# Hybrid mLSTM and differential attention block: q and k of four attention heads as seven block products each, rotated in the pairs' stage and kept in DRAM

## The chip, the cores and the metric

One core of a Trainium2 chip (trn2) runs the whole block. The metric is the time of one execution on the device, in microseconds (us); lower is better. The engines are TensorE (PE), VectorE (DVE), ScalarE (ACT), GpSimd (POOL) and SyncE (SP), which issues nearly all transfers. Each engine takes its instructions in order and waits for the others by semaphores.

## What is computed

One layer for a sequence of 1024 rows of width 1024, in float32. After a root-mean-square norm, one wide projection gives twelve segments. Five of them (a_q, a_k, a_v, a_o, a_z) and the gates a_g feed an mLSTM with 4 heads in two directions; b_q, b_k, b_v and b_z feed a differential attention with 8 heads; g_a and g_b gate the two branches. What the change touches is the attention's q and k:

```
dq = apply_rope(b_q.reshape(B, S, 8, 2, 64), positions)   # rotation of the halves (t1, t2) of 64:
dk = apply_rope(b_k.reshape(B, S, 8, 2, 64), positions)   # t1 cos - t2 sin, t2 cos + t1 sin
p = softmax(dq dk^T * 64 ** -0.5)          # for each head two maps j = 0, 1
out = (p[0] - lam * p[1]) @ da_v           # then a norm and a gate with b_z
```

## The kernel before

Every large product is made of float32r matmuls in three terms: each operand is split into a high part H and a low part L, and HH, HL and LH are added in PSUM. A projection of 128 columns by 512 rows of the sequence takes 8 slices of the depth times 3 terms, 24 matmuls with 512 columns.

*Stages.* First the norm, the transposed input (`hH`, `hL`, one tile for each half of the sequence) and four early z projections. Then the **pairs' stage**: two projections of 128 columns and both halves of the sequence and of the depth are a 2 x 2 by 2 x 2 block product, for which `pair_units` takes seven products instead of eight, of 4 x 3 = 12 matmuls each, in Winograd's form, from sums of blocks of the input (`TH`, `TL`) and of the weights. `load_form` makes the weight forms: a sum or difference on POOL, a cast to H on ACT (L354), and L by a subtraction on POOL or DVE (L358). The form of a pair's product f waits in one of six buffers until a product before is done. Products 0, 1, 2 and 6 of a pair add up in one PSUM bank, so product 6 waits until ACT has copied the sum after product 2 away (`u3`, L392). Product 6 and product 5 of a pair are issued among the next pair's. When two or three products have come together, a **sink** finishes a block (i, j): i is the one of the two projections, j the half of the sequence. Before, there are 2 wide pairs for v of the mLSTM, 16 pairs that alternate between the convolution's sink (four POOL instructions each, L560) and the o and z sink (none on POOL), and 3 gate pairs.

*The attention stage.* The plain projections of q and k of one head are `da_proj`: kA is the weight of the first halves (t1) of q and k side by side, kB that of the second (t2), each for both halves of the sequence, 96 matmuls in all (L607). `first` multiplies kA's result by cos and sin (DVE, L1045 and L1046), `second` does kB's (L1056 and L1057); POOL adds and splits (L1058 to L1062, six instructions) and SP copies the parts into `kst` and `qq` (L1067), eight copies of two instructions' worth of rows for each half.

A head then has 8 steps t. In each, `scores` makes 12 matmuls S (L1126; two of them run at once on halves of the array), DVE takes two maxima (L1129), ACT two exponentials (L1131), which free the two PSUM tiles of S, and DVE the difference e (L1137). `transposes` makes 8 transposes T of the e of the step before, ACT and DVE split them (pH L1150, pL L1151), and every second step `pv` multiplies two steps by v (L1162, 24 matmuls). There is one set of PSUM tiles for S and two banks for T, PV and the small products.

*What sets the order.* PE's order is fixed by the program (`Weaver`). It gives every unit a cost, and names after which it may come, with a delay (`LAG`): S of a head comes 14 us after the head's projection, T 6.8 us after its S. `weave` merges the head's own units with a list of other work: q and k of the next head, v of the next two heads (`da_v`, after the last PV of the head before), z of the heads that aren't early. The other engines' and SP's order is made by a scheduler from this program.

Of the kernel before, what the change touches and what calls it, by code (L numbers as in the profile page):

```python
# [38 lines left out]
Z_EARLY = (0, 1, 3, 5)  # L39
MM = 0.214  # L40
# [88 lines left out]
class Block:  # L129
# [126 lines left out]
    def pair_raws(self, p):  # L256
        if p >= len(self.pairs) or p in self.praws:
            return
        self.praws[p] = raws = []
        if self.pairs[p][0] == "v":  # L260
            pool = self.wpool if p % 2 == 0 else self.s0
            for b in range(2):
                t = pool.tile([128, 8, 128], F32, name="raw", tag="raw", **({} if p % 2 == 0 else dict(bufs=2)))
                raws.append({0: wide(t)})
                self.load_piece(p, b, 0)
            for b in (1, 0):
                self.praws[p][b][1] = self.kit[(0, 4)[p % 2] + 1 - b].rearrange("p (k e) -> p k e", e=256)
                self.load_piece(p, b, 1)
            return
        for seg, i in self.pairs[p]:  # L270
# [50 lines left out]
    def load_form(self, key):  # L321
# [5 lines left out]
        r1, r2 = self.praws[p]  # L327
# [4 lines left out]
        lo, hi = slice(0, 4), slice(4, 8)  # L332
        tmp = lambda n: self.s0.tile([128, 4, 128], F32, name=n, tag=n, bufs=1)
        sub = lambda out, x, y: g.tensor_tensor(out=out, in0=x, in1=y, op=ALU.subtract)
        if f == 0:
            src = r1[:, lo]
        elif f == 1:
            self.s2f = src = tmp("s2f")
            sub(src, self.s1f, r1[:, lo])
        elif f == 2:  # L340
            src = self.s13[:, hi]
            sub(src, r1[:, lo], r2[:, lo])
        elif f == 3:
            self.s13 = self.s0.tile([128, 8, 128], F32, name="s13", tag="s13", bufs=1)
            self.s1f = src = self.s13[:, lo]
            g.tensor_tensor(out=src, in0=r2[:, lo], in1=r2[:, hi], op=ALU.add)
        elif f == 4:
            src = r1[:, hi]
        elif f == 5:
            src = self.s2f  # L350
            sub(src, r1[:, hi], src)
        else:
            src = r2[:, hi]
        cast = a.copy(H, src)  # L354
# [3 lines left out]
        (self.v if f in (0, 4, 6) else g).tensor_tensor(out=Lo, in0=src, in1=H.bitcast(F32), op=ALU.subtract)  # L358
# [148 lines left out]
    def gate_sink(self, i0):  # L507

        def sink(i, j, ps, rest):
# [7 lines left out]
            self.q.dma_start(out=self.tg["gb"][i0 + i][:, j * 512:(j + 1) * 512], in_=th)  # L517
        return sink
# [516 lines left out]
    def da_proj(self, h, st):  # L1035
# [73 lines left out]
    def da_parts(self, h, st):  # L1109
# [79 lines left out]
        def scale(half):  # L1189
# [10 lines left out]
            S=lambda t: Unit(6 * MM, lambda: scores(t), tag="S", hold=LAG["Sh"], name=("S", h, t), after=((("qk", h), LAG["qk"]),)),  # L1200
# [480 lines left out]
    def build(self):  # L1681
# [21 lines left out]
        with pool(name="const", bufs=1) as self.const, \  # L1703
# [20 lines left out]
            self.vd = {x: [[self.dram.tile([128, 512], F32, name=f"av{x}{n}_{c}") for c in range(NC)] for n in range(NH_A)] for x in "HL"}  # L1724
            self.zd = {h: self.dram.tile([128, S], F32, name=f"zd{h}") for h in Z_EARLY}
# [4 lines left out]
            for n in range(NH_A):  # L1730
                for i, seg in enumerate(("ak", "aq")):
# [3 lines left out]
                    sinks.append(self.oz_sink(2 * n + i))  # L1735
            for n in range(0, 6, 2):
# [181 lines left out]
```

## Time and profile before

| | |
|---|---|
| median of 3 runs (lowest to highest) | 1648.4 us (1648.01 to 1649.74) |
| the profiled execution | 1648.9 us |
| its span, first to last instruction | 1647.1 us |
| mean granted clock of PE | 0.999 |
| DVE, ACT, POOL: share of the span | 63%, 48%, 41% |
| moved by DMA | 208.15 MB, mean 126 GB/s |

The profile is of one execution. A row of the timeline has the start in the span, the length, engine, line, operation, what it writes and reads, and in brackets how long the engine stood before it and what ended that. A row of a group has the busy time, the mean length of one in ns, and the idle time before. Matmuls are pipelined: one is longer than the distance to the next. The stages, by the profile: the pairs' stage until about 530 us, attention from there to about 1160, then the mLSTM and the output.

### The profile page before, as it was taken

What the parts mean: (1) busy time and instruction counts of PE and PEld (TensorE: products, weight loads), DVE (VectorE), ACT (ScalarE), POOL (GpSimd) and SP (SyncE); (2) the same over time, 40 slices, a digit from 0 to 9 for tenths busy, and PEclk for the clock granted to TensorE, in tenths of its full rate; (3) what the DMA queues carried; (4) which work ended last, traced back from release to release, by engine and by line L of the source; (5) the groups of instructions that cost most, each with busy time, mean ns of one, the idle gap of its engine ahead of it and who ended that gap; (6) DMA issues with size and microseconds to landing.
All of it is one profiled execution on the core that took longest, in us unless ns stands there. A gap on an engine that the chain in (4) does not pass through costs nothing.

```text
span 1647.1 us, 25481 instructions
## 1 busy us (share of the span) xinstructions
PE 1616.7 (98%) x9299; PEld 1364.3 (83%) x9299; DVE 1045.8 (63%) x1866; ACT 787.8 (48%) x1602; POOL 674.1 (41%) x725
## 2 busy tenths in 40 slices
PE   7999999999999999999999999999999999999998
PEld 6899778878888988987888888888898888888887
DVE  5734787786771377677767776764167867456633
ACT  6433545555553254455445444554357666442221
POOL 3744676666774446243515344322322322222000
PEclk9999999999999999999999999999999999999999
DMA  5433444343443323222222131311697863466522
GB/s 186 151 127 131 119 135 148 115 141 116 146 129 109 103 54 89 65 64 78 54 72 63 46 77 39 91 52 52 200 307 260 270 190 130 145 227 216 179 101 78
DMA packets 193167, 208.15 MB, mean 126 GB/s; under 512 B 12313, under 2 KB 143730, under 8 KB 193042
## 3 DMA queue, kind: packets, MB, share of 16 engines
q1 hardware_dynamic: 189826, 200.75, 39.5%
q10 hardware_dynamic: 3216, 5.78, 0.9%
q8 instruction: 73, 1.20, 0.3%
q14 instruction: 52, 0.43, 0.1%
HBM read 128.79 MB, written 60.92 MB: 115 GB/s over the span
## 4 chain that ended last, share of the span: by engine, by line
PE 66%; DVE 4%; ACT 2%; DMA 2%; POOL 1%; issue 1%; SPq 0%; POOLq 0%; DVEq 0%; ACTq 0%
PE pj L607 27%; PE T L385 9%; PE T L1162 6%; PE S L1126 5%; PE pj L1631 5%; PE T L159 5%; PE pj L629 5%; PE T L155 2%; PE I L155 1%; PE SS L155 1%; PE PO L155 1%; DMA raw<-in_w_in_dram 1%; DMA ya<-gA 0%; DVE e L1137 0%; DVE hL L1517 0%
## 5 line engine op out<-in xcount | busy, mean ns | idle before, releaser
L607 PE MATMUL pj<-hH,wH 128*128 128x512 f32 x672 | 274.4, 408 | 0.1
L607 PE MATMUL pj<-hH,wL 128*128 128x512 f32 x672 | 263.8, 393 | 0.8 <-POOL wL L244 0.8
L607 PE MATMUL pj<-hL,wH 128*128 128x512 f32 x672 | 263.0, 391 | 0.6 <-DVE hL L763 0.6
L1129 DVE TENSOR_REDUCE nm<-S 128x1 f32<-128x1024 f32 x128 | 150.7, 1219 | 108.7 <-PE S L1126 108.7
L607 PEld LDWEIGHTS pj<-hH,wL 128*128 128x128 f32 x672 | 126.1, 188 | 29.4 <-POOL wL L244 2.1
L1131 ACT ACTIVATE e<-S,nm 128x1024 f32<-128x1024 f32 x128 | 142.7, 1130 | 7.0 <-DVE nm L1129 7.0
L607 PEld LDWEIGHTS pj<-hL,wH 128*128 128x128 f32 x672 | 126.7, 189 | 21.7 <-DVE hL L763 1.5
L607 PEld LDWEIGHTS pj<-hH,wH 128*128 128x128 f32 x672 | 126.6, 188 | 20.2 <-ACT hH L762 0.5
L1150 ACT CAST pH<-T 128x512 fp32r<-128x512 f32 x128 | 68.8, 588 | 147.4 <-PE T L159 147.4
L246 POOL TENSOR_TENSOR wL<-raw,wH 128x1024 fp32r<-128x1024 f32 x27 | 66.6, 2466 | 121.2 <-ACT wH L238 121.2
L1126 PE MATMUL S<-kst,qq 64*128 64x512 f32 x768 | 106.2, 408 | 0.0
L385 PE MATMUL T<-TH,wL 128*128 128x512 f32 x304 | 101.2, 394 | 2.4 <-ACT u L392 2.3
L385 PE MATMUL T<-TH,wH 128*128 128x512 f32 x304 | 101.0, 392 | 0.1
L1137 DVE SCALAR_TENSOR_TENSOR e<-e,r,e 128x1024 f32<-128x1024 f32 x64 | 93.5, 1461 | 1.8
L1126 PEld LDWEIGHTS S<-kst,qq 64*128 64x128 f32 x768 | 67.3, 184 | 29.2 <-issue 9.4
L551 DVE SCALAR_TENSOR_TENSOR pj<-cin,cols,pj 128x512 f32<-128x512 f32 x128 | 87.1, 745 | 0.0
L1151 DVE TENSOR_TENSOR pL<-T,pH 128x512 fp32r<-128x512 f32 x128 | 82.0, 680 | 6.1 <-ACT pH L1150 6.1
L224 POOL TENSOR_TENSOR wL<-raw,wH 128x512 fp32r<-128x512 f32 x32 | 47.0, 1485 | 79.8 <-ACT wH L223 79.8
L607 PE MATMUL pj<-sl_yb,wH 128*128 128x512 f32 x256 | 78.9, 389 | 0.0
L385 PE MATMUL T<-hH,wH 128*128 128x512 f32 x232 | 76.5, 391 | 0.2 <-DVE cin L532 0.2
L1333 POOL TENSOR_SCALAR_AFFINE_SELECT W<-gb 128x128 f32<-128x128 f32 (+1 forms) x64 | 26.3, 414 | 122.9 <-DVE W L1383 87.0
L385 PE MATMUL T<-hH,wL 128*128 128x512 f32 x224 | 74.5, 392 | 0.7 <-DVE oz L491 0.7
(405 smaller groups left out, 4449.4 us busy)
## 6 DMA issues: line engine op xcount, KB each, us to landing
raw<-in_w_in_dram SPq DMA_DIRECT2D x84, 512.0 KB, 4.0
kst<-hl SPq DMA_DIRECT2D x64, 128.0 KB, 2.4
qq<-hl SPq DMA_DIRECT2D x64, 128.0 KB, 2.4
x<-in_x_dram SPq DMA_DIRECT2D x8, 512.0 KB, 5.7
avH<-tz SPq DMA_DIRECT2D x16, 256.0 KB, 2.0
cak<-y SPq DMA_DIRECT2D x16, 256.0 KB, 2.7
cakH<-cin SPq DMA_DIRECT2D x16, 256.0 KB, 4.8
cakL<-tz SPq DMA_DIRECT2D x16, 256.0 KB, 4.6
```

What stands on the lines that cost most here:

```text
L155: self.t.matmul(out, lhsT=l, rhs=r, start=(i == 0), stop=(i == n - 1))
L159: self.t.transpose(out, in_, self.ident[0:k, 0:k])
L385: self.t.matmul(ps, lhsT=l[:, k, :], rhs=r[:, k, :], start=(first and k == 0 and m == 0), stop=(k == 3 and m == 2), skip_group_check=not f ...
L551: v.scalar_tensor_tensor(out=acc, in0=raw[:, o + x:o + x + 512], scalar=w(x), in1=acc, op0=ALU.mult, op1=ALU.add)
L607: self.t.matmul(ps, lhsT=l[:, k, :], rhs=r, start=(n == 0), stop=(n == 23))
L629: self.t.matmul(ps[:, i, :], lhsT=l, rhs=r[:, k, :], start=(kh == 0 and k == 0 and m == 0), stop=(kh == 1 and k == 3 and m == 2))
L1126: self.t.matmul(ps[:, o], lhsT=qq[r, x, c], rhs=k[r, y, o], start=(m == 0), stop=(m == 2))
L1129: v.tensor_reduce(out=nm, in_=ps, axis=AX.X, op=ALU.max, negate=True)
L1131: a.activation(out=e, in_=ps, func=AF.Exp, bias=nm[:, 0:1], accum_out=Z[:, j, t:t + 1])
L1137: v.scalar_tensor_tensor(out=e0, in0=e, scalar=r[:, 0:1], in1=e0, op0=ALU.mult, op1=ALU.add)
L1162: self.t.matmul(ps[:, 0:256], lhsT=l[:, k, :], rhs=r[:, i, :], start=(k == 0 and m == 0), stop=(k == 7 and m == 2))
L1631: self.t.matmul(ps, lhsT=x[:, s], rhs=y[:, c], start=(k == 0 and m == 0), stop=(k == 7 and m == 2))
```

## The change

For heads 0, 2, 4 and 6 the plain projections kA and kB in the attention stage are gone. In their place each has a pair `("rope", h)` in the pairs' stage, after the 16 mLSTM pairs and before the gate pairs. The two projections of the pair are kA and kB; its weights are loaded in two pieces by halves of the depth, with q's and k's 128 columns side by side, and the forms read them in groups of 32 columns. The new `rope_sink` adds the parts, multiplies by cos and sin (DVE), adds (POOL), casts (ACT) and subtracts (DVE), and SP writes H and L to a tensor `rd` in DRAM. In the attention stage `load_qk` loads `kst` and `qq` of such a head from `rd`, k and the first half of q at the start of the head before, the second half of q after its step 3. S of these heads then comes at least 5 us after the second load by the planner, instead of 14 after a projection. The other heads are as before.

```
+R_EARLY = (0, 2, 4, 6)
...
+        if self.pairs[p][0] == "rope":
+            vw = lambda x: x.rearrange("p k (g i) -> p k g i", i=32)
+            part = lambda b, kh: wide(self.praws[p][kh]).rearrange("p k (g t i) -> p k g t i", t=2, i=32)[:, :, :, b, :]
...
+    def rope_sink(self, h):
+        v, a, p, box = self.v, self.a, self.p, {}
+        def sink(i, j, ps, rest):
+            c = slice(j * 512, (j + 1) * 512)
+            if rest is not None:
+                to = self.psA.tile([128, 512], F32, name="pj", tag="pj", bufs=2) if i == j == 1 else ps
+                v.tensor_tensor(out=to, in0=ps, in1=rest, op=ALU.add)
+                ps = to
+            t = box[i, j] = self.big("rot")[:, 0:S]
+            v.tensor_tensor(out=t[:, 0:512], in0=ps, in1=(self.sinT if i else self.cosT)[:, c], op=ALU.mult)
+            v.tensor_tensor(out=t[:, 512:S], in0=ps, in1=(self.cosT if i else self.sinT)[:, c], op=ALU.mult)
+            if (1 - i, j) not in box:
+                return
+            x, H = box[0, j], box[1, j]
+            p.tensor_tensor(out=x[:, 0:512], in0=x[:, 0:512], in1=H[:, 0:512], op=ALU.subtract)
+            p.tensor_tensor(out=x[:, 512:S], in0=H[:, 512:S], in1=x[:, 512:S], op=ALU.add)
+            a.copy(H.bitcast(F32R), x)
+            v.tensor_tensor(out=x.bitcast(F32R), in0=x, in1=H, op=ALU.subtract)
+            for n, y in enumerate((H, x)):
+                self.q.dma_start(out=self.rd[h][:, :, n, c], in_=y.rearrange("p (x s) -> p x s", x=2))
+        return sink
...
+        def load_qk(half):
+            if half == 0:
+                st["k"] = w1.tile([128, 2, S], F32R, name="kst", tag="kst", bufs=2)
+            st["q", half] = w1.tile([128, 2, 512], F32R, name="qq", tag="qq", bufs=3)
+            for x in range(2):
+                for j in range(2):
+                    r, g = 64 * j + 32 * x, 32 * j
+                    if half == 0:
+                        q.dma_start(out=fb(st["k"][r:r + 32]), in_=self.rd[h][64 + g:96 + g, x])
+                    q.dma_start(out=fb(st["q", half][r:r + 32]), in_=self.rd[h][g:g + 32, x, :, half * 512:half * 512 + 512])
...
         qk = []
-        for half in range(2):
+        if h in R_EARLY:
+            qk = [Unit(0.0, lambda: load_qk(0)), Unit(0.0, lambda: load_qk(1), name=("qk", h), after=((("S", h - 1, 3), 1.0),), lane=1)]
+        for half in range(0 if h in R_EARLY else 2):
             qk += self.proj(kA, half, lambda ps, half=half: first(half, ps))
...
-            S=lambda t: Unit(..., name=("S", h, t), after=((("qk", h), LAG["qk"]),)),
+            S=lambda t: Unit(..., name=("S", h, t), after=((("qk", h), 5.0 if h in R_EARLY else LAG["qk"]),)),
...
+            for h in R_EARLY:
+                self.pairs.append(("rope", h))
+                sinks.append(self.rope_sink(h))
```

The order that comes of it, at three places. PE, between the last S of head 0 and the first of head 1 (`S<-kst,qq`; `ident,e` are transposes T, `pj<-hH,wH` a projection, `T<-pH,vH` PV, `ident,att` the small transposes). Before, the end of it:

```order
L607 MATMUL pj<-hH_195,wH 128x512
L607 MATMUL pj<-hL_196,wH 128x512
L607 MATMUL pj<-hH_195,wL 128x512
L1126 MATMUL S<-kst,qq 128x512 x12
L159 MATMUL T<-ident,e_5919 128x128 x8
L607 MATMUL pj<-hH_195,wH 128x512
```

In the change, all of it and what follows:

```order
L1179 MATMUL S<-kst,qq 128x512 x12
L160 MATMUL T<-ident,e_6290 128x128 x8
L647 MATMUL pj<-hH_201,wH 128x512
L647 MATMUL pj<-hL_202,wH 128x512
L647 MATMUL pj<-hH_201,wL 128x512
L160 MATMUL T<-ident,att 128x128 x2
L1179 MATMUL S<-kst,qq 128x512 x12
L160 MATMUL T<-ident,e_6368 128x128 x8
L1215 MATMUL T<-pH,vH 128x256
L1215 MATMUL T<-pL,vH 128x256
L1215 MATMUL T<-pH,vL 128x256
```

Before, 42 projection matmuls stand between the two S and 12 more between T and PV; in the change three, the last of head 1's projection, and none.

POOL, in the pairs' stage (`s`, `s2f`: sums for weight forms; `wH<-s`, `wL<-s2f`: their low parts; `y<-y,cin` a convolution's sink, `rot<-rot` the rope sink). Before, one pair's turn:

```order
L346 TENSOR_TENSOR s_4415<-raw 128x512
L334 TENSOR_TENSOR s_4415<-raw 128x512
L358 TENSOR_TENSOR wH<-s_4415,wH 128x512
L560 TENSOR_TENSOR y<-y,cin 128x512 x2
L358 TENSOR_TENSOR wL<-s2f,wL 128x512
L334 TENSOR_TENSOR s2f<-s_4415,raw 128x512
L358 TENSOR_TENSOR wH<-s2f,wH 128x512
L334 TENSOR_TENSOR s2f<-raw,s2f 128x512
L560 TENSOR_TENSOR y<-y,cin 128x512
```

In the change, a rope pair's turn:

```order
L351 TENSOR_TENSOR s_5048<-raw 128x512 x2
L552 TENSOR_TENSOR rot<-rot 128x512
L553 TENSOR_TENSOR rot<-rot 128x512
L374 TENSOR_TENSOR wH<-s_5048,wH 128x512
L552 TENSOR_TENSOR rot<-rot 128x512
L553 TENSOR_TENSOR rot<-rot 128x512
L374 TENSOR_TENSOR wL<-s2f,wL 128x512
L351 TENSOR_TENSOR s2f<-s_5048,raw 128x512
L374 TENSOR_TENSOR wH<-s2f,wH 128x512
```

Four sink instructions stand in one turn in both, in the change two ahead of the first low part and two behind it, and so in four turns running.

SP, around the copies of head 1's second half (`kst<-hl`, `qq<-hl`), in the change (before, `kst<-hl` and `qq<-hl` stand there alone, behind a weight load):

```order
L202 DMA raw<-in_w_in_dram 128x8x128
L1124 DMA kst<-rd_167 32x2048 x3
L1107 DMA kst<-hl 32x2x512 x2
L1107 DMA qq<-hl 32x2x512 x2
L1107 DMA kst<-hl 32x2x512 x2
L1107 DMA qq<-hl 32x2x512 x2
L1125 DMA qq<-rd_167 32x2x512 x3
```

Three loads of head 2's k, into the buffer that head 0's k leaves, stand ahead of them.

More of the change, by code (lines that the diff above doesn't have):

```diff
@@ L269, in pair_raws @@
             return
+        if self.pairs[p][0] == "rope":
+            pool = self.wpool if p % 2 == 0 else self.s0
+            for kh in range(2):
+                t = pool.tile([128, 8, 128], F32, name="raw", tag="raw", **({} if p % 2 == 0 else dict(bufs=2)))
+                for i, seg in enumerate(("bq", "bk")):
+                    o = OFF[seg] + 128 * self.pairs[p][1]
+                    src = self.A["w_in"][0][512 * kh:512 * kh + 512, o:o + 128]
+                    self.q.dma_start(out=wide(t)[:, :, 128 * i:128 * i + 128], in_=src.rearrange("(k p) e -> p k e", p=128))
+                raws.append(t)
+            return
         for seg, i in self.pairs[p]:
@@ L326, in load_form @@
             self.pair_raws(1)
-        r1, r2 = self.praws[p]
+        if self.pairs[p][0] == "rope":
+            vw = lambda x: x.rearrange("p k (g i) -> p k g i", i=32)
+            part = lambda b, kh: wide(self.praws[p][kh]).rearrange("p k (g t i) -> p k g t i", t=2, i=32)[:, :, :, b, :]
+        else:
+            vw = lambda x: x
+            part = lambda b, kh: self.praws[p][b][:, 4 * kh:4 * kh + 4]
         tag = "wH" if self.forms % 2 == 0 else "wL"
@@ L331, in load_form, with sub @@
         H, Lo = t[:, 0:4], t[:, 4:8]
-        lo, hi = slice(0, 4), slice(4, 8)
         tmp = lambda n: self.s0.tile([128, 4, 128], F32, name=n, tag=n, bufs=1)
-        sub = lambda out, x, y: g.tensor_tensor(out=out, in0=x, in1=y, op=ALU.subtract)
+        def sub(out, x, y, op=ALU.subtract):
+            g.tensor_tensor(out=vw(out), in0=x, in1=y, op=op)
+            return vw(out)
         if f == 0:
-            src = r1[:, lo]
+            src = part(0, 0)
         elif f == 1:
-            self.s2f = src = tmp("s2f")
-            sub(src, self.s1f, r1[:, lo])
+            self.s2f = tmp("s2f")
+            src = sub(self.s2f, vw(self.s1f), part(0, 0))
         elif f == 2:
-            src = self.s13[:, hi]
-            sub(src, r1[:, lo], r2[:, lo])
+            src = sub(self.s13[:, 4:8], part(0, 0), part(1, 0))
         elif f == 3:
             self.s13 = self.s0.tile([128, 8, 128], F32, name="s13", tag="s13", bufs=1)
-            self.s1f = src = self.s13[:, lo]
-            g.tensor_tensor(out=src, in0=r2[:, lo], in1=r2[:, hi], op=ALU.add)
+            self.s1f = self.s13[:, 0:4]
+            src = sub(self.s1f, part(1, 0), part(1, 1), ALU.add)
         elif f == 4:
-            src = r1[:, hi]
+            src = part(0, 1)
         elif f == 5:
-            src = self.s2f
-            sub(src, r1[:, hi], src)
-        else:
-            src = r2[:, hi]
-        cast = a.copy(H, src)
+            src = sub(self.s2f, part(0, 1), vw(self.s2f))
+        else:
+            src = part(1, 1)
+        cast = a.copy(vw(H), src)
         if f in (1, 5):
             self.behind(self.pins.get("u"), cast)
-        (self.v if f in (0, 4, 6) else g).tensor_tensor(out=Lo, in0=src, in1=H.bitcast(F32), op=ALU.subtract)
+        (self.v if f in (0, 4, 6) else g).tensor_tensor(out=vw(Lo), in0=src, in1=vw(H.bitcast(F32)), op=ALU.subtract)
         self.wt[key] = (H, Lo)
@@ L517, in sink @@
             self.q.dma_start(out=self.tg["gb"][i0 + i][:, j * 512:(j + 1) * 512], in_=th)
+        return sink
[11 more added lines that the diff above has]
+            if (1 - i, j) not in box:
+                return
+            x, H = box[0, j], box[1, j]
[5 more added lines that the diff above has]
+                self.q.dma_start(out=self.rd[h][:, :, n, c], in_=y.rearrange("p (x s) -> p x s", x=2))
         return sink
@@ L1199, in da_parts @@
         return dict(
-            S=lambda t: Unit(6 * MM, lambda: scores(t), tag="S", hold=LAG["Sh"], name=("S", h, t), after=((("qk", h), LAG["qk"]),)),
+            S=lambda t: Unit(6 * MM, lambda: scores(t), tag="S", hold=LAG["Sh"], name=("S", h, t), after=((("qk", h), 5.0 if h in R_EARLY else LAG["qk"]),)),
             T=lambda t, g: Unit(4 * TP, lambda: transposes(t, g), tag="T", hold=LAG["Th"], name=("T", h, t, g),
@@ L1724, in build @@
             self.vd = {x: [[self.dram.tile([128, 512], F32, name=f"av{x}{n}_{c}") for c in range(NC)] for n in range(NH_A)] for x in "HL"}
+            self.rd = {h: self.dram.tile([128, 2, 2, S], F32, name=f"rd{h}") for h in R_EARLY}
             self.zd = {h: self.dram.tile([128, S], F32, name=f"zd{h}") for h in Z_EARLY}
```

## The prediction

> **What bounds the kernel now.** I read the page first, then the chain of work, then the timeline around two heads of the attention stage, then the groups of instructions of the pairs' stage.
>
> ```profile
> PE 1616.7 (98%) x9299; PEld 1364.3 (83%) x9299; DVE 1045.8 (63%) x1866; ACT 787.8 (48%) x1602; POOL 674.1 (41%) x725
> 461.48 62.63 PE T L385 x276
> 530.50 21.76 PE pj L607 x96
> 552.26 15.83 PE pj L629 x132
> ```
>
> TensorE (PE) is the bound: busy in 98% of the span, no other engine above 63%. The two pieces of the chain give the price of a matmul of 512 columns. 276 of the pairs' stage took 62.63 us and 96 of a projection 21.76 us, so 0.227 us each (the 408 ns in the page's groups is one matmul's length in a pipeline, not its pace). The 96 are head 0's whole q and k projection; the third piece is v, 0.12 us for each matmul of 256.
>
> So two things can change the time: how many matmuls there are, and whether PE still always has one whose operands are there. The attention stage shows how it has that now.
>
> ```profile
> 636.20:708.40 72.20, 71.55 (x530) 63.04 (x529) 51.53 (x72) 37.22 (x82) 28.07 (x29) 1.00 0.20 53
> 776.90:855.10 78.20, 78.20 (x560) 68.28 (x559) 53.27 (x75) 37.27 (x82) 29.15 (x30) 1.00 0.21 55
> ```
>
> These are the stretches from the first score product of heads 1 and 3 to that of the next head (PE, weight loads, VectorE (DVE), ScalarE (ACT), GpSimd (POOL), granted clock, DMA). PE is full, DVE is busy for 52 to 53 us. One step t of a head is a chain through three engines:
>
> ```profile
> 787.13 1.66 PE L1126 MATMUL S<-kst,qq 64*128 64x512 f32 x12
> 788.72 1.09 PE L159 MATMUL T<-ident,e 128*128 128x128 f32 x8
> 788.83 2.36 DVE L1129 TENSOR_REDUCE nm<-S 128x1 f32<-128x1024 f32 x2 [3.57 <-PE S L1126]
> 791.48 1.13 ACT L1131 ACTIVATE e<-S,nm 128x1024 f32<-128x1024 f32 x1
> 791.10 1.28 DVE L1151 TENSOR_TENSOR pL<-T,pH 128x512 fp32r<-128x512 f32 x2
> 793.23 1.28 DVE L1137 SCALAR_TENSOR_TENSOR e<-e,r,e 128x1024 f32<-128x1024 f32 x1
> ```
>
> With the score product S at 0: PE is free for the transposes T of the step before at 1.6; they take 1.09 with the tail of the last one, so the next matmul can start at about 2.5. The second exponential ends at 5.5, and only then are S's banks free for the next S. The weights e of this step are ready at 7.4. The low parts pL of the transposed ones are written at 4.0 to 5.3, since DVE does the two maxima first, so the product PV can't begin before about 4.6. Between 2.5 and 4.6 to 5.5 PE needs other work: the projections of the next head and v.
>
> **The change part by part.** *Matmuls.* Four heads lose 96 each and four pairs gain 7 x 12 = 84 each: 48 fewer, 48 x 0.227 = **-10.9 us**. The work also moves: 4 x 84 x 0.227 = 76.3 us come to the pairs' stage, 21.8 go from the front of the attention stage, and 3 x 21.8 = 65 from the heads before 2, 4 and 6, where they were PE's other work. The rotation's products on DVE and POOL move with them.
>
> *Head 0 to head 1.* Head 1 is not among the four, so its projection still runs beside head 0. Now nothing follows it: the planner used to put 42 matmuls of head 2's projection (9.5 us) between it and head 1's first S, and those are gone, while v for heads 2 and 3 must wait for head 0's last PV. What that S waits for is here:
>
> ```profile
> 620.39 0.39 PE L607 MATMUL pj<-hH,wL 128*128 128x512 f32 x1
> 623.77 1.66 PE L1126 MATMUL S<-kst,qq 64*128 64x512 f32 x12
> 632.89 1.23 SPq L1067 DMA_DIRECT2D kst<-hl  x2
> 636.17 1.65 PE L1126 MATMUL S<-kst,qq 64*128 64x512 f32 x12
> kst<-hl SPq DMA_DIRECT2D x64, 128.0 KB, 2.4
> 600.60 1.29 POOL L1058 TENSOR_TENSOR m<-m,hl 128x512 f32<-128x512 f32 x1 [14.34 <-DVE hl L1056]
> 605.70 1.29 POOL L1062 TENSOR_TENSOR hl<-m,hl 128x512 fp32r<-128x512 f32 x1
> 607.71 1.23 SPq L1067 DMA_DIRECT2D kst<-hl  x2
> ```
>
> Head 1's last projection matmul ends at 620.8; the last k copies are issued at 632.9 to 634.1, and the second, issued at 633.5, lands 2.4 later at 635.9 at the latest (an estimate from the median). S comes at 636.17, so this delay of some 15 us was covered, barely. In the change the last three projection matmuls stand behind S(7) and T, and end at 1.6 + 0.9 + 0.7 = 3.2, plus 0.4 of pipeline; behind them PE has two short transposes and then head 1's S, at 3.5. DVE does maxima and pL until 5.3 and then the first product with sin, 5.9. POOL's six instructions took 6.4 us in the undisturbed half at 600.60; one low part of a rope weight now stands among them, 1.4. That is 13.7. From POOL's end to the last landing are 0.7 of issue wait, 0.6 between the two issues and 2.4: 17.4. PE waits 17.4 - 3.5, about **+14 us**. From below 11, if the weight's low part and DVE's order cost nothing; from above 17, since SP now stands with three loads of head 2's k, which wait for head 0's last S, ahead of these copies.
>
> *The heads 1, 3, 5.* Their only other work is now v, 192 matmuls, which may begin after the last PV of the head before. In step 0, and again in step 6 when v is used up, the order is S, T, PV with nothing between: PE stands from 2.5 to 4.7, 2.2 us. In step 6 DVE also has two parts of v and a gate product of the step before ahead of the maxima, about 0.6 more. That is 2.2 + 2.8 = 5.0 per head, **+15 us** for three. Below: 9, if DVE is ahead; above: 20, with 0.7 more at the ends of heads 2 and 4 and a late e.
>
> *The rope pairs.* Four pairs follow one another whose sinks put four instructions on POOL (L1058's kind). Of the pairs before, only every second did.
>
> ```profile
> L346 POOL TENSOR_TENSOR s<-raw 128x512 f32<-128x512 f32 x19 | 28.2, 1483 | 1.4
> L358 POOL TENSOR_TENSOR wH<-s2f,wH 128x512 fp32r<-128x512 f32 x20 | 26.0, 1299 | 32.4 <-ACT wH L354 32.4
> L354 ACT CAST wH<-raw 128x512 fp32r<-128x512 f32 x28 | 17.4, 620 | 6.4 <-PE pj L879 3.3 <-PE T L435 2.2 <-PE T L385 0.9
> L238 ACT CAST wH<-raw 128x1024 fp32r<-128x1024 f32 x41 | 43.1, 1052 | 43.7 <-PE pj L607 26.7 <-DMA raw<-in_w_in_dram 9.1 <-issue 6.5
> L1045 DVE TENSOR_TENSOR m<-pj,cosT 128x512 f32<-128x512 f32 x16 | 11.0, 690 | 14.2 <-PE pj L607 11.8 <-POOL hl L1062 2.4
> L358 DVE TENSOR_TENSOR wL<-raw,wL 128x512 fp32r<-128x512 f32 x29 | 31.0, 1073 | 4.5 <-ACT wL L354 4.5
> ```
>
> POOL's own time per pair is 8 weight-form instructions of 1.35 and 4 of 1.3, 16.0 of the pair's 84 x 0.227 = 19.1. But in its order it also waits: after the first two rotations for ACT's copy of 1024 and two casts (1.05 + 2 x 0.62 = 2.3), then for DVE's subtraction, a low part, a sum and a product beyond that (about 1.4), after the next two for ACT's copy and a cast (1.7), and once more for a cast (0.7). 16.0 + 6.1 = 22.1 is 3 us more than PE needs, and ACT's copy u of the third product, which PE's seventh waits for, stands behind. Three of four pairs would each lose 3: 9. If casts and sinks slip past one another as in the conv pairs, nothing. The order of the change shows them in a row, so I take **+7.5**, from 0 to 14 (a subtraction of 1024 at twice 1.07 instead of 0.69 adds 1.5 per pair).
>
> *PE's pace after a long wait.* The trace of before has no gap of over 3 us once PE runs, but its beginning shows slow matmuls:
>
> ```profile
> 0.00:15.00 15.00, 6.48 (x30) 5.08 (x30) 5.77 (x23) 7.61 (x11) 7.51 (x19) 1.00 0.87 315
> 8.24 1.54 PE L159 MATMUL T<-ident,x 128*128 128x128 f32 x6 [2.33 <-DVE rsv L693]
> 13.81 0.88 PE L159 MATMUL T<-ident,x 128*128 128x128 f32 x6 [0.19 <-DVE x L705]
> ```
>
> The same six transposes take 1.54 us after PE stood for 8 us with little work, and 0.88 five microseconds later, while the granted clock of these 15 us (the last column but two) is 1.00: it doesn't show this. S and T after the 14 us wait (2.5 us) would take 2.5 x 1.54 / 0.88 = 4.3: **+1.8 us**, between 0 and 4. The Trainium skill's page "TensorE: Matmul & The Clock Gate" (Part 1: The HAM clock gate) says that the array falls to half its clock after one idle window of about 3.4 us and needs as long a stretch of work to come back; by that rule the wait costs up to half of 3.4, 1.7 us (an estimate from the page's figure), more than its length, a wait under 3.4 us costs nothing beyond it, and the sum below would be +27.3 instead of +27.4; without any such effect it would be +25.6.
>
> *The rest.* The loads of the kept q and k replace as many bytes of copies, run one head ahead, and for head 0 beside 120 matmuls of v, 14 us: nothing, unless they come more than some 3 us late. SP's wait for head 0's last S holds up only head 1's copies, priced above. The stages after attention keep their order.
>
> Sum: -10.9 + 14 + 15 + 7.5 + 1.8 = +27.4. The profiled execution took 1648.9 (its span 1647.1 and 1.8 around it), 0.5 above the median of three, 1648.4. So 1648.4 + 27.4 = **1676 us**.
>
> **The rivals.** *Only the matmul count decides* (faster). If PE finds work at every place, the time is 1648.4 - 10.9 = 1637.5. For it: PE is full now, and PE work was the bound in every stage. Against it: the order of the change has nothing to give PE at head 1, and the delay of 15 us there is in the trace. The point from which it decides: all new waits together under 10.9 us. 0.03.
>
> *Only head 1 waits.* The other heads' steps and the rope pairs hold, because S, T and v leave DVE enough lead: -10.9 + 14 + 1.8 = +4.9, 1653 us. For it: DVE has 8 x 0.69 = 5.5 us less to do per head without the rotation. Against it: pL stands behind the maxima in the order, whatever lead DVE has. 0.12.
>
> *POOL becomes the bound of the rope pairs*, with 22 to 23.5 us for each of four pairs: 14 to 18 instead of 7.5 there, 1685 us. For it: 16.0 of 19.1 us busy. Against it: some waits fall together. 0.15.
>
> *The change is paid back exactly*, waits of about 11 us: 1648.4. Head 1's wait alone is priced above it. 0.02.
>
> **How the numbers follow.** The forecast has 0.68. The range reaches from the second rival's upper part to the third's far side: low -10.9 + 11 + 9 + 0 + 0 = +9, 1657; high with the upper bounds of two of the three large terms, -10.9 + 17 + 18 + 14 + 4 = +42, 1690. About 0.2 % or 3.3 us is what a measurement of this kernel can tell from no change. Faster by more than that: 0.03, the first rival. Within it: 0.02. Slower: 0.95, the other three.
>
> **What would show it.** In the profile of the changed kernel: PE at S of head 1 with 10 us or more of idle time before it, ended by the k copies; that S and the T behind it at nearly half pace; idle time before PV in steps 0 and 6 of heads 1, 3 and 5, ended by pL; pairs of rope longer than 19.1 us with PE waiting for ACT's u. In all, 48 fewer matmuls. It is wrong if head 1's first S follows head 0's last by under 10 us, if the rope pairs hold 19.1 us, or if another head waits for its loads.

## The result, and the profile after

The changed kernel takes **1695.5 us** (median of 4 runs, 1694.0 to 1696.0) against 1648.9 us of the kernel before in the same runs (1648.0 to 1649.7): a ratio of 1.0281, 95% interval 1.0263 to 1.0299. It is slower, as forecast, but by 46.6 us and not by 27.4; the time lies above the range.

The first part of the page answers to the line shown of before: 48 matmuls fewer, and yet PE's busy time is up by 8 us, because many of them took longer.

```profile
span 1694.3 us, 25435 instructions
PE 1625.0 (96%) x9251; PEld 1371.0 (81%) x9251; DVE 1069.4 (63%) x1898; ACT 807.4 (48%) x1634; POOL 666.2 (39%) x709
```

Next the waits of PE (what it waited for, us in total, times, the longest), first from the first S of head 0 to that of head 7. Before, the same stretch had 1.7 for pL and 0.7 for e, and nothing else.

```profile
PE T L1215 <- DVE pL L1204: 13.0, 6, 2.5
PE S L1179 <- DMA kst<-hl: 11.5, 1, 11.5
PE T L160 <- DVE e L1190: 5.3, 9, 0.9
PE T L160 <- DVE pL L1204: 1.3, 1, 1.3
PE T L160 <- DVE zg L1249: 0.8, 3, 0.3
```

Then the rope pairs, which before doesn't have. The other pairs wait for u as in before, 2.3 us in all in each kernel.

```profile
PE T L401 <- ACT u L408: 8.2, 4, 2.9
```

The longest single wait of all is at the first S of head 1: six of its matmuls run straight away, the other six wait for the second half of k.

```profile
695.45 1.50 PE L1179 MATMUL S<-kst,qq 64*128 64x512 f32 x6
708.48 2.19 PE L1179 MATMUL S<-kst,qq 64*128 64x512 f32 x6 [11.53 <-DMA kst<-hl]
713.29 0.58 PE L1215 MATMUL T<-pH,vH 128*128 128x256 f32 x1 [0.73 <-DVE pL L1204]
```

The waits for pL ahead of PV, for the k copies and for u are those that the prediction named; the other three it didn't. Together they make 40.1 us, 37.7 more than before; with 10.9 us less of matmuls that is 26.8, and 20 of the 47 us are still missing. The windows show where most of them are. Each row is a stretch of the length in its second column; the next columns are PE, weight loads, DVE, ACT, POOL, granted clock of PE, DMA share, GB/s.

```profile
507.00:510.50 3.50, 1.50 (x7) 1.05 (x6) 1.77 (x3) 2.39 (x5) 2.69 (x3) 1.00 0.69 223
510.50:513.90 3.40, 3.40 (x9) 2.65 (x8) 1.46 (x4) 0.32 (x2) 3.32 (x3) 0.50 0.25 74
513.90:517.30 3.40, 3.40 (x16) 2.81 (x15) 2.28 (x3) 0.54 (x1) 3.40 (x4) 1.00 0.00 0
712.10:718.60 6.50, 5.77 (x28) 5.37 (x27) 3.53 (x6) 3.02 (x6) 0.00 (x0) 0.50 0.11 23
981.40:984.90 3.50, 1.25 (x10) 1.25 (x11) 3.35 (x7) 2.84 (x6) 1.08 (x1) 1.00 0.28 60
984.90:988.30 3.40, 3.40 (x18) 3.40 (x17) 1.17 (x1) 0.16 (x1) 0.00 (x0) 0.51 0.00 0
988.30:991.70 3.40, 3.40 (x31) 3.40 (x30) 0.00 (x0) 0.21 (x1) 1.29 (x1) 0.99 0.02 5
```

The first three rows are a rope pair. PE stood for 2.0 of the first 3.5 us; in the next 3.4 us it is full, but does 9 matmuls where the third row has 16, and the granted clock says 0.50. The last three are step 0 of head 5: PE stands, then 18 matmuls in 3.4 us, then 31. So **PE can run at half its pace for 3.4 us after it has stood for little more than 2**. I summed, over all such stretches, how much longer each matmul's distance to the next is than the same matmul's median in the profile of before: eight stretches (from 510.6, 555.2, 710.9, 713.7, 768.9, 902.8, 985.1 and 1038.4 us) cost 1.6, 1.4, 0.6, 2.2, 2.0, 1.6, 1.4 and 2.1, together **13.0 us**. The six S matmuls that follow head 1's wait aren't in this sum; they cost about 1 us more. Before has no such stretch between its beginning and its last 2.1 us. Some 6 us of the 20 are left: PE's new start after each wait, 0.3 to 0.5 us in the rows where it can be read, is part of them; they weren't added up one by one.

The same sum by stage: the four turns of the rope pairs last 88.7 us (490.8 to 579.5) for 4 x 19.1 = 76.3 of matmuls, 12.4 too much. The time in the attention stage beyond its matmuls at the pace of before has grown by 2.5 us in head 0, 23.3 in head 1, 9.1 in head 3 and 11.3 in head 5, and fallen by 1.2 in heads 2, 4 and 6 together: 45.0. With the 12.4 and -10.9 that makes 46.5 of the 47.2 us by which the span is longer. Heads 1, 3 and 5, in the columns of above:

```profile
695.50:781.30 85.80, 69.82 (x486) 61.25 (x485) 51.46 (x74) 38.53 (x89) 22.29 (x23) 0.84 0.22 60
844.20:915.00 70.80, 64.50 (x486) 56.95 (x485) 50.69 (x73) 38.95 (x90) 15.66 (x17) 0.98 0.22 59
977.90:1050.80 72.90, 66.61 (x485) 59.13 (x485) 50.65 (x73) 38.91 (x90) 15.64 (x17) 0.93 0.19 51
```

Step 6 of head 3, where the forecast had only the wait for pL, on PE (rows with waits and the S around them), then DVE and POOL in the same stretch:

```profile
890.06 1.66 PE L1179 MATMUL S<-kst,qq 64*128 64x512 f32 x12
...
896.21 1.65 PE L1179 MATMUL S<-kst,qq 64*128 64x512 f32 x12
898.73 0.63 PE L160 MATMUL T<-ident,e 128*128 128x128 f32 x4 [0.88 <-DVE e L1190]
899.63 0.66 PE L160 MATMUL T<-ident,e 128*128 128x128 f32 x4 [0.27 <-DVE zg L1249]
902.83 0.43 PE L1215 MATMUL T<-pH,vH 128*128 128x256 f32 x1 [2.54 <-DVE pL L1204]
907.37 0.96 PE L1179 MATMUL S<-kst,qq 64*128 64x512 f32 x6
```

```profile
896.17 2.42 DVE L1190 SCALAR_TENSOR_TENSOR e<-e,r,e 128x1024 f32<-128x1024 f32 x1
```

```profile
896.21 3.51 POOL L225 TENSOR_TENSOR wL<-raw,wH 128x512 fp32r<-128x512 f32 x2 [4.30 <-ACT wH L224]
```

Step 6 takes 907.37 - 896.21 = 11.2 us for S, T and PV, 5.1 us of work. Step 5 had run out of v and was only 6.15 us long (896.21 - 890.06), so e of step 5, ready 7.4 us after its S in the best case, has hardly any time to spare; and it took 2.42 us where the row shown of before has 1.28, with two of POOL's low parts beside it, which took 3.51 instead of 2 x 1.3. With 1.28 it would have been ready at 897.45, when S of step 6 still ran until 897.86: the wait needs both, the short step and the slow e. Then come the pL wait, and 17 matmuls at half pace.

### The profile page after: what moved, and what is told of

Read it like the earlier page. It is cut to its first block, busy times and chain, and to the rows that moved or that the text cites. A ratio compares the mean times of both kernels' runs of the same rounds, so it can differ in the third digit from the quotient of the medians.

```text
span 1694.3 us, 25435 instructions
## 1 busy us (share of the span) xinstructions
PE 1625.0 (96%) x9251; PEld 1371.0 (81%) x9251; DVE 1069.4 (63%) x1898; ACT 807.4 (48%) x1634; POOL 666.2 (39%) x709
## 3 DMA queue, kind: packets, MB, share of 16 engines
q1 hardware_dynamic: 192514, 209.14, 40.1%
## 4 chain that ended last, share of the span: by engine, by line
PE 56%; DVE 8%; POOL 4%; issue 3%; ACT 3%; DMA 3%; SPq 0%; POOLq 0%; DVEq 0%; ACTq 0%
PE pj L647 17%; PE T L401 9%; PE T L1215 6%; PE S L1179 5%; PE pj L1684 5%; PE pj L669 5%; PE T L160 5%; PE I L156 1%; PE T L156 1%; DMA bm<-bd 1%; DVE nm L1182 1%; DVE e L1190 1%; PE SS L156 1%; PE PO L156 1%; POOL s L351 1%
## 5 line engine op out<-in xcount | busy, mean ns | idle before, releaser
L647 PE MATMUL pj<-hH,wH 128*128 128x512 f32 x544 | 222.8, 409 | 0.1
L647 PE MATMUL pj<-hH,wL 128*128 128x512 f32 x544 | 213.7, 393 | 0.8 <-POOL wL L245 0.8
L647 PE MATMUL pj<-hL,wH 128*128 128x512 f32 x544 | 213.0, 391 | 0.6 <-DVE hL L803 0.6
L401 PE MATMUL T<-TH,wL 128*128 128x512 f32 x368 | 124.8, 400 | 7.3 <-ACT u L408 7.2
L647 PEld LDWEIGHTS pj<-hH,wL 128*128 128x128 f32 x544 | 102.1, 188 | 24.0 <-POOL wL L245 2.1
L1179 PE MATMUL S<-kst,qq 64*128 64x512 f32 x768 | 109.1, 411 | 11.7 <-DMA kst<-hl 11.5
L647 PEld LDWEIGHTS pj<-hL,wH 128*128 128x128 f32 x544 | 102.6, 189 | 17.7 <-DVE hL L803 1.4
L647 PEld LDWEIGHTS pj<-hH,wH 128*128 128x128 f32 x544 | 102.5, 188 | 16.4 <-ACT hH L802 0.5
L401 PEld LDWEIGHTS T<-TH,wL 128*128 128x128 f32 x368 | 70.3, 191 | 26.4 <-ACT u L408 11.8
L1215 PE MATMUL T<-pH,vH 128*128 128x256 f32 x256 | 76.9, 300 | 13.0 <-DVE pL L1204 13.0
L401 PEld LDWEIGHTS T<-TH,wH 128*128 128x128 f32 x368 | 69.3, 188 | 19.2 <-ACT u L408 4.6
```

Source lines behind the costliest of these rows:

```text
L401: self.t.matmul(ps, lhsT=l[:, k, :], rhs=r[:, k, :], start=(first and k == 0 and m == 0), stop=(k == 3 and m == 2), skip_group_check=not f ...
L647: self.t.matmul(ps, lhsT=l[:, k, :], rhs=r, start=(n == 0), stop=(n == 23))
L1179: self.t.matmul(ps[:, o], lhsT=qq[r, x, c], rhs=k[r, y, o], start=(m == 0), stop=(m == 2))
L1215: self.t.matmul(ps[:, 0:256], lhsT=l[:, k, :], rhs=r[:, i, :], start=(k == 0 and m == 0), stop=(k == 7 and m == 2))
```

## The experiments

The theory that I formed from this: the loss is waits at the three places that the prediction named, and PE's half pace after each longer stand, which multiplies them; all of it goes where PE has other work, or where the wait is taken away. Rivals: the rope pair or the loads through DRAM cost by themselves; the slow stretches come from DVE, ACT or the transfers; the attention stage, with so much of PE's work gone, is bound by the chain of DVE and ACT wherever the rest of it lies.

**Rope pairs and gate pairs by turns.**

```
-            for h in R_EARLY:
-                self.pairs.append(("rope", h))
...
+            for kind, n in (("rope", 0), ("gb", 0), ("rope", 2), ("gb", 2), ("rope", 4), ("rope", 6), ("gb", 4)):
```

> The four rope pairs no longer stand in a row: the order is rope 0, gate, rope 2, gate, rope 4, rope 6, gate. The changed kernel takes 1695.5 us, and its seven pairs from the first rope pair on cost 12 us more than 84 matmuls each (waits of 8.8 us for ACT's copy u, and 3.0 us at half pace behind two of them). Theory 1 (POOL's turn of 16 us plus its waits is too long when one rope pair follows another): a gate pair gives POOL its time back, only the one doubled place (rope 6 behind rope 4) still waits 2 to 3 us, and the time falls by 6 to 9 us, to about 1688. Theory 2 (each rope pair is too long by itself, by its casts and sums): all four still wait, the time stays at 1694 to 1697.

Measured: 1692.9 us, ratio to before 1.0269 (1.0253 to 1.0284), far from theory 1's 1688 and 1 us under theory 2's range. The 2.6 us are little, and the waits stayed:

```profile
PE T L401 <- ACT u L408: 7.8, 4, 2.6
```

8.2 us in the changed kernel, 7.8 here. By theory 1 only rope 6, behind rope 4, would wait; it is the one that waits least (0.7 us), and the three others wait 2.6, 2.5 and 2.0. So theory 2 holds: a rope pair is too long without a rope pair beside it. What was gained is half pace, which these stands happened not to set off (below).

**Work in the stands.**

```
+        def junk():
+            ps = self.psA.tile([128, 512], F32, name="pj", tag="pj", bufs=2)
+            for n in range(10):
+                self.t.matmul(ps, lhsT=self.hH[0][:, n % 8, 0:128], rhs=self.hH[0][:, n % 8, :], ...)
...
+        if cur and cur["h"] in (1, 3, 5) and t in (0, 6):
+            un.append(Unit(0.0, cur["junk"]))
```

> Between T and PV in steps 0 and 6 of heads 1, 3 and 5, where PE stands for 1.0 to 2.7 us in the changed kernel, ten matmuls of 512 columns are added whose sum nobody reads (10 x 0.227 = 2.3 us at each of six places, 13.6 us of PE work more). Theory 1 (PE falls to half its pace because it stood): the stretches of some 3 to 5 us at half pace behind these stands go away (7.2 us in all at steps 6 of heads 1, 3, 5 and step 0 of head 5), the added work lies within the stands, and the time FALLS by 4 to 8 us to about 1689 although there is more work. Theory 2 (the slow stretches come from something else there, such as DVE, ACT or the transfers, or are only the way the trace models matmuls): the time stays at 1695 or grows by what doesn't fit the stands, up to 1700.

Measured: 1689.9 us, 1.0252 (1.0237 to 1.0267): 5.6 us less with 13.6 us of matmuls more. The same place as above in head 5, step 0: PE, then the window behind it.

```profile
978.95 1.06 PE L160 MATMUL T<-ident,e 128*128 128x128 f32 x8 [0.26 <-DVE e L1190]
979.76 2.52 PE L1255 MATMUL pj<-hH 128*128 128x512 f32 x10
982.31 0.39 PE L1215 MATMUL T<-pH,vH 128*128 128x256 f32 x1
```

```profile
984.90:988.30 3.40, 3.40 (x31) 3.40 (x30) 0.00 (x0) 0.37 (x1) 1.29 (x1) 1.00 0.00 0
```

PV begins as late after T as without the ten matmuls, and then runs at full pace, 31 matmuls in 3.4 us. Heads 3 and 5 went from 70.9 and 73.1 us to 69.3 each, with 20 matmuls more. Standing is the cause of the pace; DVE, ACT and the transfers did the same work in both. The gain in the attention stage is larger than the 5.6 us: the rope pairs, which the edit doesn't touch, had three windows at half pace here instead of two, and head 0 began 3.3 us later (636.3 against 633.0).

**Head 0 alone.**

```
-R_EARLY = (0, 2, 4, 6)
+R_EARLY = (0,)
```

> Only head 0 has the change, heads 2, 4 and 6 are projected in the attention stage as before. Theory 1 (the loss lies in what is taken from heads 2, 4 and 6, where the projection was PE's other work, and in rope pairs that follow one another): 12 matmuls fewer are 2.7 us, one rope pair before a gate pair costs 0 to 2, head 1's first S has head 2's projection ahead of it again: 1645 to 1648, not slower than before (1648.4). Theory 2 (the rope pair or the loads through DRAM cost by themselves): a quarter of the loss of 47 stays, 1655 to 1661.

Measured: 1656.7 us, 1.0046 (1.0029 to 1.0063). That is within theory 2's 1655 to 1661; but the loss doesn't lie where theory 2 alone would have it. PE's waits from the rope pair to head 1:

```profile
PE T L401 <- ACT u L408: 3.3, 2, 2.6
PE T L1215 <- DVE pL L1204: 2.6, 1, 2.6
PE pj L647 <- DVE m L1086: 1.7, 1, 1.7
```

The rope pair does cost by itself, its wait and the half pace that it set off (1.6 us), and no wait is for a load from `rd`. The second wait, with half pace behind it (1.2 us), is new: in step 2 of head 0, ACT stood behind casts of the weights of head 1's q and k (L224), whose loads had not come. That it is the missing projection in front of head 0 that makes them late is argued, not shown.

**A gate projection ahead of v in head 1.**

```
-FILL = (0, 0, 0, 0, 0, 0, 0, 2)
+FILL = (0, 1, 0, 0, 0, 0, 0, 1)
...
-                    nxt = ahead + self.da_v((h + 1) // 2, sts[h + 1:h + 3]) + fill(FILL[h])
+                    nxt = ahead + fill(FILL[h]) + self.da_v((h + 1) // 2, sts[h + 1:h + 3])
```

> All four heads have the change; one of the two gate projections that run beside head 7 (48 matmuls, 10.9 us) is put ahead of v in head 1 instead, so that it stands between the last projection of head 1 and its first S and again PE has work there. Heads 3 and 5 stay as they are. Theory 1 (head 1's 25 us over its work are a lack of other work, the wait for the k copies of 11.8 us, the stands in steps 0 and 6, and half pace behind them): the wait shrinks to 1 to 3 us, head 1's excess to 4 to 8 us, head 7 loses nothing: 1673 to 1680. Theory 2 (the copies come as late as the work is long, since SP stands with the loads of head 2 ahead of them): the gain is no more than the moved work's 10.9 us, and a wait for k of 5 us or more stays: 1684 or more.

Measured: 1686.3 us, 1.0223 (1.0208 to 1.0239). The wait for the k copies is 3.9 us instead of 11.5, and the time of heads 0 and 1 beyond their work fell by 15.5, less than the 17 to 21 of theory 1. All 48 matmuls stood ahead of head 1's first S, so step 0 behind it still had nothing, which I had overlooked. Head 7 lost 3.2 us with one gate fewer:

```profile
PE S L1179 <- DMA kst<-hl: 3.9, 1, 3.9
```

```profile
PE T L1215 <- DVE pL L1204: 2.3, 2, 1.3
```

The mechanism is theory 1's, the time is within theory 2's: a stand filled with work from another head is paid for there.

**The rope sink's sums on DVE.**

```
-            p.tensor_tensor(out=x[:, 0:512], ..., op=ALU.subtract)
-            p.tensor_tensor(out=x[:, 512:S], ..., op=ALU.add)
+            v.tensor_tensor(out=x[:, 0:512], ..., op=ALU.subtract)
+            v.tensor_tensor(out=x[:, 512:S], ..., op=ALU.add)
```

> The changed kernel, with the rope sink's subtraction and sum on DVE instead of POOL (16 instructions of 512 columns in all). Theory 1 (POOL's turn of a rope pair is longer than PE's 19 us, and ACT's copy u stands behind a cast that waits for POOL; with a gate pair on either side a rope pair still waited 2.1 to 2.7 us): POOL's turn falls by 4 x 1.3 = 5.2 us to about 17, the waits for u of 8.8 us in the four pairs fall to 0 to 2, half pace behind them goes, and the time falls by 7 to 12 us to 1684 to 1689. Theory 2 (ACT and DVE are the long ones: DVE takes over 4 to 5 us per pair and its own subtractions come later): u comes as late as before, 1693 or more.

Measured: 1681.5 us, 1.0199 (1.0184 to 1.0214), 14.0 less than the changed kernel, more than theory 1's 7 to 12. The four turns of the rope pairs, in the changed kernel and here:

```profile
490.80:579.50 88.70, 80.54 (x338) 65.07 (x337) 46.36 (x60) 31.15 (x50) 67.17 (x48) 0.96 0.43 142
```

```profile
491.00:567.10 76.10, 76.10 (x337) 63.08 (x336) 57.46 (x76) 32.07 (x50) 47.11 (x32) 1.00 0.52 166
```

16 instructions fewer on POOL, and 12.6 us go: PE is full. Why POOL was late is to be read on ACT in the changed kernel, which takes its instructions in order:

```profile
503.27 1.05 ACT L554 CAST rot<-rot 128x1024 fp32r<-128x1024 f32 x1 [3.54 <-POOL rot L553]
504.23 0.61 ACT L370 CAST wL<-s2f 128x512 fp32r<-128x512 f32 x1
508.11 0.62 ACT L370 CAST wH<-s2f 128x512 fp32r<-128x512 f32 x1 [3.27 <-POOL s2f L351]
508.63 0.58 ACT L408 COPY u<-T 128x512 f32<-128x512 f32 x1
```

The sum of PE's third product had long been there when ACT copied it at 508.63: ACT waited for POOL's rotation until 503.27 and for POOL's next weight sum until 508.11. PE's product that needs the bank came at 509.27. With the sums on DVE the same copy began at 504.9, in a turn that started 0.2 us later.

**z of the odd heads beside the odd heads**, and with it the sums on DVE.

```
-Z_EARLY = (0, 1, 3, 5)
+Z_EARLY = (0, 2, 4, 6)
...
-                    nxt = ahead + self.da_v(...) + fill(FILL[h])
+                    nxt = z[h] + ahead + self.da_v(...) + fill(FILL[h])
...
-                    nxt = z[h - 1] + ahead + fill(FILL[h]) + z[h] if h else v0[20:] + ahead + fill(FILL[0])
+                    nxt = ahead + fill(FILL[h]) + z[h] if h else v0[20:] + ahead + fill(FILL[0])
```

The edit also moves the place in z that waits for the gate of the head before, takes z in a lane of its own, and changes the buffers of z's gate from 2 to 3 and of its load from 2 to 1.

> The changed kernel, with the early z projections for heads 0, 2, 4, 6 instead of 0, 1, 3, 5, so that heads 1, 3 and 5 have 48 matmuls of z (10.9 us) ahead of v, and heads 2, 4 and 6 lose as many (one more buffer for z's gate, one fewer for its load). No matmul more or fewer. Theory 1 (PE stands where a step has no other work): head 1's wait of 11.8 us falls to 2 to 4 since 36 matmuls stand behind its projection, heads 3 and 5 lose their 20 us of stands and half pace, while heads 2, 4 and 6 now have a step 5 and a step 6 without other work and stand 3 to 6 us each: the time falls by 12 to 26, to 1670 to 1684. Theory 2 (the attention stage is bound by the chain of DVE and ACT when so much of PE's work has left, wherever the rest lies): what the odd heads gain the even ones lose, 1690 to 1700.

> Both edits: the rope sink's sums on DVE, and z in heads 1, 3 and 5. If the two costs lie in different stages they add up: by theory 1 of each 1658 to 1675; more than 5 us above the sum of the two single gains would speak for a cost that both share.

Measured: 1720.4 us, 1.0434 (1.0416 to 1.0451), and with the sums on DVE 1705.4, 1.0348 (1.0332 to 1.0363). The two edits add up (-14.0 and +24.9 from 1695.5 give 1706.4). But the second is no test of what it was made for, since it brought a wait of its own:

```profile
PE pj L669 <- DVE vL L1162: 24.5, 6, 4.7
```

The last piece of z's half waits for the gate of the head before, and until then holds one of the two banks `pj`; v, left with one, waited for its eviction. Steps 0 and 6 of heads 3 and 5 did lose their waits. But heads 2, 4 and 6 got 7.6, 8.4 and 8.7 us longer beyond their work, in steps 5 and 6 above all, where theory 1 had 3 to 6; rid of the bank, the experiment might have come out either way.

**Head 4 alone, with the sums on DVE and a gate projection ahead of v in head 3**, the gate taken from head 7, or from the mLSTM's stage.

```
-R_EARLY = (0, 2, 4, 6)
+R_EARLY = (4,)
...
+FILL = (0, 0, 0, 1, 0, 0, 0, 1)        # the other kernel: (0, 0, 0, 1, 0, 0, 0, 2)
```

> Only head 4 has the change, its sums are on DVE, and one of head 7's two gate projections stands ahead of v in head 3, in the place of head 4's projection (48 matmuls for the 96). 12 matmuls fewer are 2.7 us. Theory 1 (the rope pair costs nothing once POOL's turn is short enough, and attention loses nothing as long as each step has other work): heads 3 to 6 keep their pace, head 7 stands some 3 us with one gate fewer, as it did where head 1 got that gate: 1646 to 1650, no slower than before. Theory 2 (each early head costs by itself, as head 0 alone seemed to, 8 us): 1655 or more.

> The kernel with head 4 alone (1649.1 us, no different from before), but head 7 keeps both of its gate projections, so that the one for head 3 comes from the mLSTM's stage, which has four instead of five to fill it. If the mLSTM's stage can spare it, head 7's 3.3 us of waits go and the 12 matmuls fewer show: 1644.5 to 1647 (0.1 to 0.2% under before). If that stage needs it, PE stands there instead: 1648 to 1656.

Measured: 1649.1 us, 1.0005 (0.9995 to 1.0014), no difference from before; and 1656.9, 1.0052 (1.0038 to 1.0066) where the mLSTM's stage gave the gate. So an early head need not cost anything: with the sums on DVE and a gate in the projection's place the pair keeps 19.0 us, heads 3 to 6 keep their pace, and the 2.7 us of 12 matmuls pay for head 7's waits. Taken from the mLSTM's stage, the gate leaves a wait there that before doesn't have (others grow, and a window at half pace follows at 1439.5 us); the time is 1 us above the range forecast for that case:

```profile
PE T L160 <- ACT hm L1470: 3.7, 1, 3.7
```

**The same work in another order**, with the sums on DVE.

```
+                    if h + 1 in R_EARLY:
+                        nxt[-4].after = ((("S", h, 6), 0.0),)        # the last 24 matmuls of v
...
+                if h in (2, 4) and h + 2 in R_EARLY:
+                    nxt, kept_z = nxt[:-2], nxt[-2:]                 # the last 6 of z
+                    kept_z[0].after = ((("S", h + 1, 0), 0.0),)
```

> The kernel with the rope sink's sums on DVE (1681.5 us), and the same instructions in another order: the last four pieces of v (24 matmuls) wait for S of step 6 in heads 1, 3 and 5, and the last two pieces of z of heads 2 and 4 (6 matmuls) stand behind the first S of heads 3 and 5, between T and PV. Theory 1 (the stands are a matter of where the other work lies): step 6 of the three heads loses its 2.7 us and the half pace behind it, 4 to 6 us each, step 0 of heads 3 and 5 falls under the 2 us of standing that half pace seems to need, 1 to 3 us each; step 5 with less v and step 7 of heads 2 and 4 with less z give back 0 to 1 us each: 1662 to 1670. Theory 2 (it is the amount of PE's work: with 65 us taken away a head lasts as long as the chain of DVE and ACT): 1679 to 1683.

Measured: 1669.0 us, 1.0116 (1.0101 to 1.0132), 12.4 less with the same instructions. Heads 3 and 5 went from 73.2 and 70.9 to 67.1 and 67.2. PE's waits in the attention stage until head 7:

```profile
PE S L1179 <- DMA kst<-hl: 11.5, 1, 11.5
PE T L160 <- DVE pL L1204: 5.8, 6, 2.0
PE T L160 <- DVE e L1190: 4.2, 8, 0.9
PE T L1215 <- DVE pL L1204: 4.0, 7, 1.0
```

The wait for pL ahead of PV fell from 13.0 to 4.0, and 5.8 came back ahead of T and the small transposes, where step 5 now has less; but in pieces of 1 us, and heads 3 and 5 have no stretch at half pace any more. So the order is worth 12 us; what remains in heads 3 and 5, some 3 us each above the heads that are full, I put down to a lack of work; no run shows it by itself. The chain of DVE and ACT alone doesn't ask for 67 us: heads 2 and 4 pass the same eight steps in 62.1.

**Work in all the stands**, with the sums on DVE: as the second experiment, and 50 matmuls ahead of head 1's first S.

```
+                if h == 1:
+                    w.add(do(lambda: cur["junk"](50)))
```

> The kernel with the rope sink's sums on DVE (1681.5 us), with 50 matmuls that nobody reads ahead of head 1's first S, where PE waits 11.8 us for the k copies, and ten between T and PV in steps 0 and 6 of heads 1, 3 and 5: 25 us of work more, all of it where PE stands. What is left is the waits without half pace. Theory 1: the 8.9 us of half pace in its attention stage and about 1 us of head 1's first S at half pace go: 1670 to 1674. Theory 2 (the pace has nothing to do with standing): 1681 or more.

Measured: 1674.8 us, 1.0157 (1.0143 to 1.0171), 6.7 us less with 25 us of work more, a little short of the forecast; the mean granted clock is 0.999 again, as before, and no stretch at half pace is left before the last 2 us, which before has too. The wait for k behind the 50 matmuls (11.4 us) is still 2.6 us. The copies let S go on 18.4 us after the last S of head 0, against 18.1 without the matmuls, so they came hardly later; but the matmuls also fill the 1.3 us that PE stood for pL ahead of the small transposes, and the first six S took 0.97 us instead of 1.70.

**Heads 4 and 6 alone**, with the sums on DVE, v and z held back as above.

```
-R_EARLY = (0, 2, 4, 6)
+R_EARLY = (4, 6)
```

> Only heads 4 and 6 have the change, the sums are on DVE, and v and z are held back as in the kernel before the last (heads 3 and 5). 24 matmuls fewer are 5.4 us. Theory 1: head 1 has head 2's projection again, the rope pairs cost nothing, heads 3 and 5 keep some 1 to 4 us of stands each: 1643 to 1650, the best that this theory can offer without moving work from other stages. Theory 2 (an early head costs about 8 to 9 us by itself): 1660 or more.

Measured: 1653.2 us, 1.0023 (1.0014 to 1.0033), above theory 1's 1643 to 1650 and under theory 2's 1660. No stretch at half pace, no wait in the rope pairs, head 1 as before; heads 3 and 5 are 4.4 and 4.1 us longer beyond their work than in before, head 2 1.1: more than the 5.4 us of matmuls saved. No version beat the kernel before.

## Why the prediction was wrong, point by point

- *48 matmuls, -10.9.* Right: 9251 instead of 9299.
- *Head 1's wait, +14, and S and T behind it at half pace, +1.8.* Right in place and cause: S went on 18.1 us after the last S of head 0, where 17.4 was forecast. The first step of head 1 is 27.6 us long for 9.4 of work; 14 + 1.8 + 2.2 for pL were forecast beyond the work, 18.2 came. That these agree so well is in part luck: the wait is 11.5, with 1.3 for pL ahead of it, half pace 2.8 and about 1 more in S, and the wait for pL behind it 0.7. The wait is ended by `kst<-hl`, and went where another head's work stood ahead of S.
- *Steps 0 and 6 of heads 1, 3 and 5, +15.* **This step failed.** Place and releaser were right, and the waits for pL themselves are 13.0 us. But the three heads lost 27.9 there (9.1 and 11.3 in heads 3 and 5, 23.3 - 15.8 in head 1). The prediction put it that "a wait under 3.4 us costs nothing beyond it", by a rule, and priced the clock only behind the one long wait. The runs showed 1.4 to 2.1 us of half pace behind four of the five stands that aren't in the shadow of that wait, and it went when matmuls filled them, though PV came no earlier. That is 7.1 of the 12.9 us by which the term was short. The second omission is step 6's wait for e and for zg, 0.9 and 0.3 us with 0.3 to 0.5 us to start again each time: I had not seen that step 5, in which v runs out, leaves e next to no time to spare, and took 1.28 us for an e that took 2.42 beside POOL. The trace of before has it at 2.42 us too, in four places; PE waited for it once, 0.4 us.
- *Head 0, nothing.* 2.5 us, waits for e in step 6 and pL in step 7, the same lack of work as in the other heads.
- *The rope pairs, +7.5, from 0 to 14.* Right in cause (POOL's turn, ACT's copy u behind it, shown by moving 16 instructions), mis-sized: 12.4 us, since all four pairs waited (2.2, 1.5, 3.1 and 2.1 us, by the matmuls around them) where I let three, and half pace added 3.0. I took that a pair waits because rope pairs follow one another; they do so singly too.
- *Half pace in all, +1.8.* **13.0**, and about 1 more in head 1's S. Of the 19 us that the forecast was short, 11 are this; they are the same microseconds as in the points above, told by their cause. The range failed with it: its upper end had 4 us for this term.
- *The rest, 0.* Loads of kept q and k cost nothing: heads 2, 4 and 6 start without a wait of over 0.1 us for `rd`.

The rivals: "only head 1 waits" fell by the waits for pL; "POOL becomes the bound" came near in the pairs' stage, with 22.2 us for a pair and 12.4 in all where it had 14 to 18, but its 1685 had the rest at the forecast's sizes.

The Trainium skill's page "TensorE: Matmul & The Clock Gate" (Part 1: The HAM clock gate) also says that the window is free-running. The traces agree, with 3.41 us; they differ in how much idleness it takes, and there the measurement decides.

## What to carry to other kernels

Moving work off the bound engine to another stage saves its count only where something else fills its place: list, for each step that loses work, what the engine does until the next operand comes, and price a stand of 2 us or more at up to 1.5 to 2 us above its length, since PE may run at half pace behind it. Spread what is left of the filling work over all steps (the same instructions in another order were worth 12 us here) before moving more away. And put a sink's instructions on the engine whose turn has room: look at the in-order engines that the bound engine waits for (ACT here), and at what stands ahead of the one instruction it needs.

## What the runs showed of the hardware

- *The clock works on a grid.* In the trace's record of the granted clock after, the stretches at half pace between the beginning and the last 3 us last 3.41, 3.42, 20.48, 6.83, 3.41, 3.42 and 6.83 us, so one, one, six, two, one, one and two times 3.413. They end at 513.90, 558.28, 718.70, 773.32, 906.43, 988.36 and 1042.97 us: 13, 60, 76, 115, 139 and 155 times 3.413 after the first. Four traces (the changed kernel, rope and gate pairs by turns, head 0 alone, the gate ahead of v) can be cut into windows on this grid, and PE's work in each counted at full pace, transposes included. Of the windows at full clock, from 20 us on and without the last 6 us, the 21 that half pace followed held at most 1.32 us of work; of the others one held 1.28 and the rest 1.46 or more. So it is how little PE does in such a window that sets off half pace, and it need not stand for all of it. A stand of 2 us costs nothing or some 1.5 us, by where it falls: in the same step 0, head 3 kept its pace and head 5 didn't, and the rope pairs' stands cost 3.0 us of half pace in the changed kernel and none with the pairs by turns, at nearly the same waits.
- *The granted clock shows it* at these places (0.50 and 0.51 in the windows above). The 1.00 beside the slow transposes at the beginning of the profile before, of which the prediction said that it doesn't show this, is no reading: the trace's record of the clock begins at 13.4 us.
- *DVE and POOL take turns on some instructions.* The difference e took 1.27 to 1.29 us in all 34 places of the trace after where POOL ran nothing beside it. Beside one of POOL's sums or low parts, the one that came second was longer by about what the first still had to do: an e that began with 1.16 us of POOL's `hl` to go took 2.24, e of step 5 above took 2.42 beside a low part of 1.30, and the low part behind that took 2.25. POOL's short instructions on `rb_v` cost e nothing (1.28).
